# Four output units added onto their residual rows by DMA, and more turns for the recurrent units

## The chip, the cores and the metric

The kernel runs on one core of a Trainium2 chip. The metric is the device time of one execution in microseconds. Three timed executions of the kernel before gave 1637.43, 1637.99 and 1639.67.

## The reference

A two-layer encoder over 512 tokens of width 2048, all in float32:

```
for layer in (0, 1):
    hn = rmsnorm(x, norm_gain[layer])
    out = even_layer(hn) if layer == 0 else odd_layer(hn)
    x = x + out
return rmsnorm(x, final_gain)

even_layer: proj = hn @ w_in -> q, k, v, g_attn, x_lru, g_lru
    attn = softmax attention, 8 heads in 2 groups, rotary positions
    xc   = convolution of width 4 over x_lru, + bias
    y    = rg_lru(xc, forward) + rg_lru(xc, backward)   # gates r, i; h = a*h + u along the tokens
    out  = concat(attn * silu(g_attn), y * silu(g_lru)) @ w_out
odd_layer:  proj = hn @ w_in -> q, k, v, o, z, gates
    h    = mlstm(forward) + mlstm(backward)             # 8 heads, chunks of 128 tokens
    out  = (rmsnorm(sigmoid(o) * h, norm_gain) * silu(z)) @ w_out
```

## The kernel before

Features lie on the 128 partitions and tokens along a row, so x is 16 feature tiles of 128 x 512, handled in eight chunks of two. Every float32 operand is split into a rounded high part and a rest (`split`, L152: ScalarE casts the high part, VectorE subtracts for the low part), and a product is three matmuls (`mm3`).

*Steps and loads.* The whole program is one list of groups (`run_steps`), each of eight chunks of the contraction. `ahead` loads weight chunks (`raw`, three buffers, all on the SP queue) and splits them (`wh`, `wl`, four buffers) a few chunks before TensorE uses them. A group's `pre` runs with the splits, its `evac` empties the PSUM banks behind the last chunk, and its `after` adds new side work.

*Lanes.* Side work (attention, recurrent units, mLSTM heads) is written as generators in two lanes; `pump(lane)` runs the next step of a lane. In a plain group lane 0 gets a turn behind bank 1 of each chunk (or behind the banks in `turns`), and lane 1 gets `pace` turns at a chunk's end. Lane 1 of layer 1 holds the four recurrent units (`lru_gen`), each of 13 steps: two convolutions, four gate products, four steps of elementwise work, and the scans (L919 to L923). The groups of layer 1 run in the order keys and values, Q[0], L[0], L[1], Q[1], GL[0], GL[1], GA[0], GA[1], where Q are the queries, L the recurrent inputs, GL the gates of the recurrent units and GA those of attention; then four output groups. `mix_split` needs the gated values in the order 0, 1, 4, 5, 6, 7, 2, 3, where 4 to 7 are the recurrent units; where one is not there, `drain_until` runs the lane's rest at once. A value that is ready before its gate is parked in memory (`mixd`) and loaded again.

*Layer 2's output projection.* Output rows come as eight units of 256 features. Group 0 makes units 0 and 1 plainly (`out2_evac`). Units 2 to 6 are seven-product groups (`run_w7`, lay `W7`): POOL forms sums of weight blocks (`w7s`, L361), both parts are split, and per chunk 21 matmuls of 256 columns go to four banks; `w7_plain` (L483 to L493) combines these in VectorE while the next unit runs, one piece a chunk, from the deque `later`. For each of these units the residual rows are loaded from `x2d` (`res_pre`, L951), added (L1365), squared (L1393), summed over the features into one accumulator `acc` (L1395, on POOL for tiles 4 to 13), scaled with the final gain (L1375) and parked in memory (`x3_store`, L1380), since the operands of the projection fill 32 of 37 large buffers. Unit 6 is kept.

*The last group* (`run_last`) loads the parked units back (L1407) and makes unit 7 in two forms: as rows for tokens 0 to 255 and as columns for tokens 256 to 511, in two halves u = 0 and 1. Behind the rows, `rows_norm` forms the factor of tokens 0 to 255 from `acc` and the last squares, spreads it over the partitions by a matmul (`rB`) and scales and stores all units; `columns_norm` does the same for each half of the other tokens, with the squares of unit 7 taken along the row and those of the other features by `others`.

Instructions are put in order for each engine by the framework's scheduler, in program order with a simulated clock; `high_priority` moves some ahead.

Of the kernel before, what the change touches and what calls it, by code (L numbers as in the profile page):

```python
# [19 lines left out]
P = 128  # L20
# [7 lines left out]
NEG = -1e30  # L28
SLOT = 1032
O7, V7 = (0, 1, 2, 3), (0,)  # L30
PACE = 2
TURNS = (0, 1, 2)
STD = 'V1 V2 V3'
NSLOT = 37

PB_BA, PB_BX, PB_LAM, PB_CW, PB_CB = 0, 16, 32, 48, 80
# [5 lines left out]
class Builder:  # L42
# [255 lines left out]
    def run_steps(self, groups):  # L298
        self.steps = [(g, c) for g in groups for c in range(NCH)]
        self.raw, self.wsp = {}, {}  # L300
        self.nload = self.nsplit = 0
        self.ahead(0, 2, 1)
        i = 0
        for g in groups:
            if g["lay"] == "W7":
                self.run_w7(g, i)
                i += NCH
                continue
            if g["lay"] == "W7c":
                self.run_w7c(g, i)  # L310
                i += NCH
                continue
            g["ps"] = [None] * 4
            while self.later:
                self.evac_later()
            if g["lay"] == "last":
                self.run_last(g, i)
                i += NCH
                continue
            for c in range(NCH):  # L320
                self.ahead(i, 3, 2)
                g["c"] = c
                ws = self.wsp.pop(i)
                for b in range(g.get("nb", 4)):
                    if c == 0:
                        g["ps"][b] = self.bank.tile([P, 512], F32, tag="bulk", name=self.name("bk"))
                    self.bulk_mm(g, g["ps"][b], g["x"](c), ws, b, c)
                    if (c < NCH - 1 or b < 1 and "turns" in g) and b in g.get("turns", (1,)):
                        self.pump(0)
                    if c == NCH - 1 and b == 0 and g.get("mid"):  # L330
                        g["mid"]()
                if c == NCH - 1:
                    with self.tc.high_priority(offset=100):
                        for b in range(g.get("nb", 4)):
                            g["evac"](b, g["ps"][b])
                    if g.get("after"):
                        g["after"]()
                    self.pump(0)
                self.pump(1, g.get("pace", 1))
                i += 1  # L340


# [51 lines left out]
    def run_w7(self, g, i):  # L394
        beside = g["f"] % 2 == 0
        pool, tag = (self.bank, "bulk") if beside else (self.aux, "aux")
        if not beside:
            self.drain_until(0, lambda: not self.held)
        ps = [None] * 4

        def product(n, c):
            a, kind, q, b, hf = self.W7[n]
            wh, wl = self.wsp[i + c]
            xh, xl = g["x"](c)[kind]
            out = self.cols7(ps[b], b, hf)
            xh, xl = (t[:, q, :].rearrange("p (q s) -> p q s", q=2) for t in (xh, xl))
            last = c == NCH - 1 and (b == 3 or hf == 1)
            self.mm3(out, wh[:, a, :], wl[:, a, :], xh, xl, c == 0 and hf == 0, last)

        for c in range(NCH):  # L410
            self.ahead(i + c, 4, 3)
            if c == 0:
                ps = [pool.tile([P, 512], F32, tag=tag, name=self.name("s7")) for _ in range(4)]
            if g.get("apart") and c >= NCH - 2:
                if c == NCH - 1:
                    for b in (0, 1, 3, 2):
                        for k in (c - 1, c):
                            for n in range(7):
                                if self.W7[n][3] == b:
                                    product(n, k)  # L420
                        self.w7_plain(g, b, ps[b])
                    self.wsp.pop(i + c - 1)
                    self.wsp.pop(i + c)
                continue
            for n in range(7):
                product(n, c)
            if c == NCH - 1:
                self.later.extend(partial(self.w7_plain, g, b, ps[b]) for b in (0, 1, 3, 2))
            self.wsp.pop(i + c)
            if c < NCH - 1:  # L430
                self.evac_later()
            if beside and c % 3 == 1:
                self.pump(0)
        if g.get("after"):
            g["after"]()

# [549 lines left out]
class Layer2(Layer1):  # L986
# [368 lines left out]
    def out2_evac(self, b, ps):  # L1355
# [3 lines left out]
        if b % 2:  # L1359
            self.x3_store(b // 2)  # L1360

    def out2_7(self, i):
        def part(t, j):
            x3 = self.xres[i][:, j, :]
            self.nc.vector.tensor_add(x3, x3, t[:, j, :])  # L1365
            self.out2_scale(2 * i + j)
            if j and i < 6:
                self.x3_store(i)

        return lambda t: self.later.extend(partial(part, t, j) for j in range(2))  # L1370

    def out2_scale(self, k):
        x3 = self.xres[k // 2][:, k % 2, :]
# [25 lines left out]
    def run_last(self, g, i0):  # L1399
# [2 lines left out]
        nc, v = self.nc, self.nc.vector  # L1402
        for c in range(NCH):
            self.ahead(i0 + c, 1, 0)
        for n in sorted(self.x3d):
            self.xres[n] = self.slot2("xres")
            nc.sync.dma_start(out=self.xres[n], in_=self.x3d[n])  # L1407
        gf = self.slot("gfrow")[:, 0:256]
        nc.sync.dma_start(out=gf, in_=self.a["gf_row"].partition_broadcast(P))

# [37 lines left out]
                out=self.a["out"][2 * i * P:(2 * i + 2) * P, cs].rearrange("(j p) s -> p j s", p=P),  # L1448
                in_=self.xres[i][:, :, cs])

        def scale(n, i, cs, rb):
            x3 = self.xres[i][:, :, cs]
            eng, r = (nc.gpsimd, rb[1]) if i in (1, 4) else (v, rb[0])
            eng.tensor_tensor(out=x3, in0=x3, in1=r.unsqueeze(1).to_broadcast([P, 2, cs.stop - cs.start]),
                              op=ALU.mult)
            store(n, i, cs)

        def columns(u, between):
            ps = self.bank.tile([P, 512], F32, tag="bulk", name=self.name("bk"))[:, 0:256]
            ts = slice(u * P, (u + 1) * P)  # L1460
            for k in range(KT):
                if k in (1, 5):
                    next(between)
                wh, wl = self.wsp[i0 + k // 4 * 2]
                xh, xl = self.h_op(k // 2, k % 2, 1)
                self.mm3(ps, xh[:, ts], xl[:, ts], wh[:, k % 4, :], wl[:, k % 4, :], k == 0, k == KT - 1)
                if k == 0:
                    for j in range(2):
                        self.mm(ps[:, j * P:(j + 1) * P], self.xres[7][:, j, 256 + u * P:256 + (u + 1) * P],
                                self.ident, start=False, stop=False)  # L1470
            return ps

        def others(u):

# [6 lines left out]
        def columns_norm(u, ps, s):  # L1481
            t = self.slot("x3c")[:, 0:256]
            nc.scalar.activation(t, ps, AF.Square, accum_out=s[:, 1:2])
            v.scalar_tensor_tensor(out=s[:, 0:1], in0=s[:, 1:2], scalar=1.0 / D, in1=s[:, 0:1],
                                   op0=ALU.mult, op1=ALU.add)
            r = self.small(1, "r3c", 2)
            self.rsqrt_short(r, s[:, 0:1], 1)
            yield
            rb = spread(r, 1)
            cs = slice(256 + u * P, 256 + (u + 1) * P)  # L1490
            for i in range(7):
                scale(i, i, cs, rb)
                if i == 2:
                    v.scalar_tensor_tensor(out=t, in0=ps, scalar=r, in1=gf, op0=ALU.mult, op1=ALU.mult)
                    nc.sync.dma_start(out=self.a["outc"][u * P:(u + 1) * P, :], in_=t)
            yield

        step = rows_norm(rows())
        s = others(0)
        step = columns_norm(0, columns(0, step), s)  # L1500
        s = others(1)
        for _ in columns_norm(1, columns(1, step), s):
            pass


    def build(self):
# [49 lines left out]
        def after_lru(g):  # L1556
# [2 lines left out]
                add(1, self.lru_gen(2 * g + 1))  # L1559
            return f  # L1560

        L = [grp(w1, 2560 + 512 * g, "T", x1, self.xlru_evac(g), after=after_lru(g)) for g in range(2)]
        Q = [grp(w1, 512 * g, "tok", x1, self.q_evac(g), after=after_q(g)) for g in range(2)]
        GA = [grp(w1, 1536 + 512 * g, "T", x1, self.gate_evac(2 * g)) for g in range(2)]
        GL = [grp(w1, 3584 + 512 * g, "T", x1, self.gate_evac(4 + 2 * g)) for g in range(2)]
        groups += [Q[0], L[0], L[1], Q[1], GL[0], GL[1], GA[0], GA[1]]

        order = [0, 1, 4, 5, 6, 7, 2, 3]
# [29 lines left out]
        SQ = [s7(1024 * w + 256 * p, 2 * (p - 1) + w, lambda t, p=p, w=w: self.qk_store(p, w, t))  # L1598
              for p in range(1, 4) for w in range(2)]
        SZ = [s7(6144 + 256 * f, 6 + f, self.z7_evac(f)) for f in range(6)]  # L1600
        Z3 = grp(w2, 6144 + 1536, "T", x2, self.z_evac, turns=TURNS, pace=PACE)
        V = [grp(w2, 2048 + 512 * p, "tok", x2, self.v_evac(p), after=after_v(p)) for p in range(4)]
        O = [grp(w2, 4096 + 512 * p, "tok", x2, self.o_evac(p), after=lambda p=p: add(1, self.hT_gen(p)))
             for p in range(4)]
# [27 lines left out]
        def late2(c):  # L1632
            if c < NCH - 1:
                h_next()

        groups[-1]["pre"] = early2
        groups.append(grp(wo2, 0, "T", hx, self.out2_evac, turns=TURNS, pace=PACE,
                          pre=self.res_pre((0, 1), self.x2d, late2)))
        groups += [dict(w=wo2[:, 256 * i:256 * i + 256], lay="W7", f=i + 1, order=range(NCH), x=self.hs.__getitem__,
                        evac=self.out2_7(i), pre=self.res_pre((i,), self.x2d)) for i in range(2, 7)]  # L1640
        groups.append(dict(w=wo2[:, 1792:2048], lay="last", order=range(NCH), pre=self.res_pre((7,), self.x2d)))
        self.run_steps(groups)

# [95 lines left out]
```

## Time and profile before

| | |
|---|---|
| median of three executions | 1637.99 us |
| the profiled execution, its own time | 1640.25 us |
| span of its profile | 1638.2 us |
| TensorE busy | 1611.1 us, 98% |
| VectorE, ScalarE, POOL busy | 1137.2, 846.6, 751.7 us |
| mean granted clock of TensorE | 0.996 |

In the rows, PE is TensorE, PEld its weight loads, DVE VectorE, ACT ScalarE, POOL GpSimd and SP the SyncE queue; a q behind the name is the engine's queue, where DMAs are issued. A row of the waits gives the waiting instruction, what ended the wait, the total in us, how often, and the longest. A row of grouped instructions gives the count, the busy time, the mean in ns, and the idle time before them. A row of the timeline gives start, duration and what was done. Matmuls overlap in the pipeline, so their pace is read from start to start and not from the duration.

### The profile page before, as it was taken

What the parts mean: (1) busy time and instruction counts of PE and PEld (TensorE: products, weight loads), DVE (VectorE), ACT (ScalarE), POOL (GpSimd) and SP (SyncE); (2) the same over time, 40 slices, a digit from 0 to 9 for tenths busy, and PEclk for the clock granted to TensorE, in tenths of its full rate; (3) what the DMA queues carried; (4) which work ended last, traced back from release to release, by engine and by line L of the source; (5) the groups of instructions that cost most, each with busy time, mean ns of one, the idle gap of its engine ahead of it and who ended that gap; (6) DMA issues with size and microseconds to landing.
All of it is one profiled execution on the core that took longest, in us unless ns stands there. A gap on an engine that the chain in (4) does not pass through costs nothing.

```text
span 1638.2 us, 25397 instructions
## 1 busy us (share of the span) xinstructions
PE 1611.1 (98%) x9698; PEld 1423.2 (87%) x9698; DVE 1137.2 (69%) x1714; ACT 846.6 (52%) x1392; POOL 751.7 (46%) x728
## 2 busy tenths in 40 slices
PE   9999999999998999999999999999999999999997
PEld 7888888888887888889999999999988888878997
DVE  8755476856755333548998896666776676688995
ACT  6334665667663333434444444444566566565542
POOL 5220122302031111576688778888521312468881
PEclk9999999999999999999999999999999999999999
DMA  7433133322324446634444444444654344443346
GB/s 231 133 93 98 52 103 103 92 89 65 116 78 151 170 168 201 193 111 118 129 120 140 129 130 117 136 135 129 193 180 130 105 154 154 158 151 116 130 157 219
DMA packets 138842, 220.22 MB, mean 134 GB/s; under 512 B 9936, under 2 KB 62544, under 8 KB 138720
## 3 DMA queue, kind: packets, MB, share of 16 engines
q1 hardware_dynamic: 137488, 217.99, 42.4%
q8 instruction: 76, 1.25, 0.3%
q10 hardware_dynamic: 1232, 0.60, 0.1%
q14 instruction: 46, 0.38, 0.1%
HBM read 184.46 MB, written 34.11 MB: 133 GB/s over the span
## 4 chain that ended last, share of the span: by engine, by line
PE 83%; DVE 7%; POOL 3%; issue 2%; ACT 2%; DMA 2%; SPq 0%; DVEq 0%; POOLq 0%; ACTq 0%
PE bk L157 47%; PE s L157 26%; DVE wl L154 3%; PE PV L157 1%; PE lg L157 1%; PE nb L157 1%; PE nf L157 1%; PE S L157 1%; PE tr L160 1%; POOL w7s L361 1%; PE ST L157 1%; PE gt L157 0%; DMA raw<-in_odd_w_out_dram 0%; POOL hfb L1323 0%; DVE ltau L919 0%
## 5 line engine op out<-in xcount | busy, mean ns | idle before, releaser
L154 DVE TENSOR_TENSOR wl<-raw,wh 128x1024 fp32r<-128x1024 f32 (+3 forms) x333 | 367.3, 1105 | 254.9 <-ACT wh L153 252.8
L153 ACT CAST wh<-raw 128x1024 fp32r<-128x1024 f32 (+3 forms) x333 | 265.7, 799 | 397.7 <-PE bk L157 189.9
L361 POOL TENSOR_TENSOR w7s<-raw 128x256 f32<-128x256 f32 x216 | 222.3, 1048 | 101.7 <-DMA raw<-in_odd_w_in_dram 55.3
L154 DVE TENSOR_TENSOR wl<-w7s,wh 128x512 fp32r<-128x512 f32 (+1 forms) x176 | 206.7, 1174 | 7.5 <-ACT wh L153 7.5
L157 PE MATMUL s<-th,wl 128*128 128x256 f32 x544 | 154.0, 283 | 4.4 <-DVE wl L154 4.4
L157 PE MATMUL s<-tl,wh 128*128 128x256 f32 x544 | 152.7, 281 | 0.0
L157 PE MATMUL s<-th,wh 128*128 128x256 f32 x544 | 152.5, 280 | 0.0
L157 PE MATMUL bk<-xh,wh 128*128 128x512 f32 x384 | 151.7, 395 | 0.0
L157 PE MATMUL bk<-xl,wh 128*128 128x512 f32 x384 | 151.3, 394 | 0.0
L157 PE MATMUL bk<-xh,wl 128*128 128x512 f32 x384 | 151.1, 393 | 0.0
L153 ACT CAST wh<-w7s 128x512 fp32r<-128x512 f32 (+1 forms) x176 | 125.7, 714 | 45.5 <-POOL w7s L361 45.4
L899 POOL TENSOR_TENSOR li<-li,xc 128x512 f32<-128x512 f32 x16 | 21.6, 1371 | 213.3 <-ACT li L891 213.3
L361 POOL TENSOR_TENSOR w7s<-w7s,raw 128x256 f32<-128x256 f32 x108 | 117.8, 1091 | 0.0
L157 PE MATMUL s<-bh,wl 128*128 128x256 f32 x408 | 115.1, 282 | 2.0 <-DVE wl L154 2.0
L157 PE MATMUL s<-bh,wh 128*128 128x256 f32 x408 | 115.2, 282 | 0.0
L157 PE MATMUL s<-bl,wh 128*128 128x256 f32 x408 | 114.6, 281 | 0.0
L361 POOL TENSOR_TENSOR w7s<-raw,w7s 128x256 f32<-128x256 f32 x108 | 105.0, 972 | 7.8
L157 PEld LDWEIGHTS s<-th,wl 128*128 128x128 f32 x544 | 102.4, 188 | 6.8 <-DVE wl L154 6.8
L157 PE MATMUL bk<-oh,wh 128*128 128x512 f32 x256 | 101.8, 398 | 5.0 <-DVE gate L805 5.0
L157 PEld LDWEIGHTS s<-tl,wh 128*128 128x128 f32 x544 | 102.5, 189 | 0.0
L157 PEld LDWEIGHTS s<-th,wh 128*128 128x128 f32 x544 | 102.5, 188 | 0.0
L157 PE MATMUL bk<-oh,wl 128*128 128x512 f32 x256 | 101.5, 396 | 0.0
(342 smaller groups left out, 4537.7 us busy)
## 6 DMA issues: line engine op xcount, KB each, us to landing
raw<-in_odd_w_in_dram SPq DMA_DIRECT2D x120, 512.0 KB, 3.9
raw<-in_even_w_in_dram SPq DMA_DIRECT2D x71, 512.0 KB, 3.7
raw<-in_even_w_out_dram SPq DMA_DIRECT2D x32, 512.0 KB, 3.6
raw<-in_odd_w_out_dram SPq DMA_DIRECT2D x32, 512.0 KB, 3.7
xres<-in_xT_dram SPq DMA_DIRECT2D x8, 512.0 KB, 6.7
x2d<-xres SPq DMA_DIRECT2D x8, 512.0 KB, 4.9
xgd<-xg SPq DMA_DIRECT2D x8, 512.0 KB, 4.5
xr<-xgd SPq DMA_DIRECT2D x8, 512.0 KB, 6.6
```

What stands on the lines that cost most here:

```text
L153: self.nc.scalar.copy(h, x)
L154: (eng or self.nc.vector).tensor_tensor(out=l, in0=x, in1=h.bitcast(F32), op=ALU.subtract)
L157: self.nc.tensor.matmul(out, a, b, start=start, stop=stop)
L160: self.nc.tensor.transpose(out, x, ident)
L361: po.tensor_tensor(out=s[:, :, q, :], in0=x, in1=y, op=op)
L899: nc.gpsimd.tensor_tensor(out=ii[j][:, d, :], in0=ii[j][:, d, :], in1=xc[:, j, :], op=ALU.mult)
```

## The change

1. *Turns.* A new key `more` gives lane 1 a turn behind bank 1 of the first `more` chunks of a group, besides the one at each chunk's end. Q[1], GL[0] and GL[1] get five; the last gate group of layer 2 (Z3) and group 0 of the output projection get eight, in place of `pace=2`.
2. *Accumulating DMA.* Units 2 to 5 no longer load their residual rows. Their combined tile is added onto the rows of `x2d` in memory by a DMA that POOL issues (`out2_onto`). From chunk 3 of unit 6 on, units 0 to 4 are loaded back, one a chunk (`x3_load`); unit 5 is loaded in the last group.
3. *Squares and scales.* The rows of units 2 to 5 are squared and scaled in the last group (`late_square`, `late_scale`), in two halves of 256 tokens; VectorE adds the squares of the first half to `acc`, POOL those of the second.
4. *The end.* `others` moves into the column products, at step 10 of 16. The factor of a column half is formed at high priority. In the second half the seven scaled tiles go into two packed buffers, and two stores take the place of seven.

```diff
-PACE = 2
+LATE = (2, 3, 4, 5)
...
+                    if b == 1 and c % 8 < g.get("more", 0):
+                        self.pump(1)
...
-                self.pump(1, g.get("pace", 1))
+                self.pump(1)
...
+            if g.get("each"):
+                g["each"](c)
...
+    def out2_onto(self, i):
+        return lambda t: self.nc.gpsimd.dma_start(out=self.rows2(self.x2d, i), in_=t, accum_op=ALU.add)
+
     def out2_7(self, i):
...
-            if j and i < 6:
-                self.x3_store(i)
...
+    def x3_load(self, i):
+        self.xres[i] = self.slot2("xres")
+        self.nc.sync.dma_start(out=self.xres[i], in_=self.x3d[i] if i in self.x3d else self.rows2(self.x2d, i))
+
+    def late_square(self, i, cs):
+        sq = self.half("sq3").rearrange("p (j s) -> p j s", j=2)
+        self.nc.scalar.activation(sq, self.xres[i][:, :, cs], AF.Square)
+        eng = self.nc.gpsimd if cs.start else self.nc.vector
+        for j in range(2):
+            eng.tensor_tensor(out=self.acc[:, cs], in0=self.acc[:, cs], in1=sq[:, j, :], op=ALU.add)
+
+    def late_scale(self, i, cs):
+        for k in (2 * i, 2 * i + 1):
+            x3 = self.xres[i][:, k % 2, cs]
+            self.nc.scalar.activation(x3, x3, AF.Copy, scale=self.pb[:, PB_GF + k:PB_GF + k + 1])
...
+        for n in range(7):
+            if n not in self.xres:
+                self.x3_load(n)
...
+                if k == 10:
+                    s = others(u)
...
+            with self.tc.high_priority(offset=100):
+                v.scalar_tensor_tensor(out=s[:, 0:1], in0=s[:, 1:2], scalar=1.0 / D, in1=s[:, 0:1],
+                                       op0=ALU.mult, op1=ALU.add)
+                self.rsqrt_short(r, s[:, 0:1], 1)
...
+            packed = [self.slot("x3p")[:, 0:1024].rearrange("p (i j s) -> p i j s", i=4, j=2) for _ in range(2 * u)]
             for i in range(7):
-                scale(i, i, cs, rb)
+                scale(i, i, cs, rb, packed[i // 4][:, i % 4] if u else None)
+                if u and i in (3, 6):
+                    (nc.scalar if i == 3 else nc.sync).dma_start(
+                        out=self.a["out"][i // 4 * 1024:(i + 1) * 256, cs].rearrange("(k p) s -> p k s", p=P),
+                        in_=packed[i // 4][:, 0:i % 4 + 1].rearrange("p i j s -> p (i j) s"))
...
+        h0, h1 = slice(0, 256), slice(256, 512)
+        for cs in (h0, h1):
+            for n in LATE:
+                self.late_square(n, cs)
+        for n in LATE:
+            self.late_scale(n, h0)
         step = rows_norm(rows())
...
+        for n in LATE:
+            self.late_scale(n, h1)
+        step = columns_norm(0, *columns(0, step))
+        for _ in columns_norm(1, *columns(1, step)):
...
-        Q = [grp(w1, 512 * g, "tok", x1, self.q_evac(g), after=after_q(g)) for g in range(2)]
+        Q = [grp(w1, 512 * g, "tok", x1, self.q_evac(g), after=after_q(g), more=5 * g) for g in range(2)]
-        GL = [grp(w1, 3584 + 512 * g, "T", x1, self.gate_evac(4 + 2 * g)) for g in range(2)]
+        GL = [grp(w1, 3584 + 512 * g, "T", x1, self.gate_evac(4 + 2 * g), more=5) for g in range(2)]
...
-        Z3 = grp(w2, 6144 + 1536, "T", x2, self.z_evac, turns=TURNS, pace=PACE)
+        Z3 = grp(w2, 6144 + 1536, "T", x2, self.z_evac, turns=TURNS, more=NCH)
...
+        groups += [u7(i, self.out2_onto(i)) for i in LATE]
+        groups.append(u7(6, self.out2_7(6), pre=self.res_pre((6,), self.x2d),
+                         each=lambda c: self.x3_load(c - 3) if c > 2 else None))
```

More of the change, by code (lines that the diff above doesn't have):

```diff
@@ L1366, in part, with rows2 @@
             self.out2_scale(2 * i + j)
-            if j and i < 6:
-                self.x3_store(i)
         return lambda t: self.later.extend(partial(part, t, j) for j in range(2))
+    def rows2(self, d, i):
+        return d[2 * i * P:(2 * i + 2) * P, :].rearrange("(j p) s -> p j s", p=P)
+    def x3_load(self, i):
[11 more added lines that the diff above has]
+            self.nc.scalar.activation(x3, x3, AF.Copy, scale=self.pb[:, PB_GF + k:PB_GF + k + 1])
     def out2_scale(self, k):
@@ L1404, in run_last @@
             self.ahead(i0 + c, 1, 0)
-        for n in sorted(self.x3d):
-            self.xres[n] = self.slot2("xres")
-            nc.sync.dma_start(out=self.xres[n], in_=self.x3d[n])
+        for n in range(7):
+            if n not in self.xres:
+                self.x3_load(n)
         gf = self.slot("gfrow")[:, 0:256]
@@ L1449, in store, with scale @@
                 in_=self.xres[i][:, :, cs])
-        def scale(n, i, cs, rb):
+        def scale(n, i, cs, rb, to=None):
             x3 = self.xres[i][:, :, cs]
             eng, r = (nc.gpsimd, rb[1]) if i in (1, 4) else (v, rb[0])
-            eng.tensor_tensor(out=x3, in0=x3, in1=r.unsqueeze(1).to_broadcast([P, 2, cs.stop - cs.start]),
-                              op=ALU.mult)
-            store(n, i, cs)
+            eng.tensor_tensor(out=x3 if to is None else to, in0=x3, op=ALU.mult,
+                              in1=r.unsqueeze(1).to_broadcast([P, 2, cs.stop - cs.start]))
+            if to is None:
+                store(n, i, cs)
         def columns(u, between):
@@ L1470, in columns @@
                                 self.ident, start=False, stop=False)
-            return ps
+            return ps, s
         def others(u):
@@ L1483, in columns_norm @@
             nc.scalar.activation(t, ps, AF.Square, accum_out=s[:, 1:2])
-            v.scalar_tensor_tensor(out=s[:, 0:1], in0=s[:, 1:2], scalar=1.0 / D, in1=s[:, 0:1],
-                                   op0=ALU.mult, op1=ALU.add)
             r = self.small(1, "r3c", 2)
-            self.rsqrt_short(r, s[:, 0:1], 1)
+            with self.tc.high_priority(offset=100):
+                v.scalar_tensor_tensor(out=s[:, 0:1], in0=s[:, 1:2], scalar=1.0 / D, in1=s[:, 0:1],
+                                       op0=ALU.mult, op1=ALU.add)
+                self.rsqrt_short(r, s[:, 0:1], 1)
             yield
@@ L1496, in columns_norm @@
             yield
+        h0, h1 = slice(0, 256), slice(256, 512)
[4 more added lines that the diff above has]
+            self.late_scale(n, h0)
         step = rows_norm(rows())
[L1499 to L1502, printed above, removed]
+        for n in LATE:
+            self.late_scale(n, h1)
+        step = columns_norm(0, *columns(0, step))
+        for _ in columns_norm(1, *columns(1, step)):
             pass
@@ L1636, in build, with u7 @@
         groups[-1]["pre"] = early2
-        groups.append(grp(wo2, 0, "T", hx, self.out2_evac, turns=TURNS, pace=PACE,
+        groups.append(grp(wo2, 0, "T", hx, self.out2_evac, turns=TURNS, more=NCH,
                           pre=self.res_pre((0, 1), self.x2d, late2)))
-        groups += [dict(w=wo2[:, 256 * i:256 * i + 256], lay="W7", f=i + 1, order=range(NCH), x=self.hs.__getitem__,
-                        evac=self.out2_7(i), pre=self.res_pre((i,), self.x2d)) for i in range(2, 7)]
+        def u7(i, evac, **kw):
+            return dict(w=wo2[:, 256 * i:256 * i + 256], lay="W7", f=i + 1, order=range(NCH), x=self.hs.__getitem__,
+                        evac=evac, **kw)
+        groups += [u7(i, self.out2_onto(i)) for i in LATE]
+        groups.append(u7(6, self.out2_7(6), pre=self.res_pre((6,), self.x2d),
+                         each=lambda c: self.x3_load(c - 3) if c > 2 else None))
         groups.append(dict(w=wo2[:, 1792:2048], lay="last", order=range(NCH), pre=self.res_pre((7,), self.x2d)))
```

## The prediction

> **What bounds the kernel now.** I read the page first, then TensorE's waits, then the chain of waits and the timelines around the two places that it shows, and last the windows by stage.
>
> ```profile
> span 1638.2 us, 25397 instructions
> PE   1611.1 (98%) x9698; PEld 1423.2 (87%) x9698; DVE 1137.2 (69%) x1714; ACT 846.6 (52%) x1392; POOL 751.7 (46%) x728
> PE s L157 <- DVE wl L154: 6.5, 11, 1.1
> PE bk L157 <- DVE gate L805: 5.0, 1, 5.0
> PE rB L157 <- DVE diag L596: 3.1, 2, 2.9
> PE nf L157 <- ACT hfb L1320: 1.4, 1, 1.4
> PE hT L160 <- ACT hfb L1190: 1.1, 3, 0.5
> ```
>
> TensorE is the bound: 1611.1 of 1638.2 us. A change can win only idle TensorE time, stretches of lower clock, and the tail behind the last matmul. One wait of 5.0 us stands alone, where the last gate group of layer 1 hands over to its output projection:
>
> ```profile
> 498.01 0.40 PE L157 MATMUL bk<-xh,wl 128*128 128x512 f32 x1
> 503.39 0.77 PE L157 MATMUL bk<-oh,wh 128*128 128x512 f32 x1 [4.99 <-DVE gate L805]
> 487.91 3.40 DVE L919 TENSOR_TENSOR_SCAN ltau<-lr,li 128x512 f32<-128x512 f32 x1 [2.31 <-POOL li L914]
> 498.01 1.23 DVE L828 TENSOR_TENSOR y<-y,gate 128x1024 f32<-128x1024 f32 x1 [1.19 <-POOL y L923]
> 502.56 2.48 DVE L805 TENSOR_TENSOR gate<-bk,rB 128x512 f32<-128x512 f32 x4
> 498.00:503.40 5.40, 0.41 (x3) 0.04 (x1) 5.38 (x6) 2.45 (x3) 0.00 (x0) 0.74 0.55 170
> 503.40:507.40 4.00, 4.00 (x10) 3.14 (x11) 2.78 (x4) 3.24 (x5) 0.00 (x0) 0.50 0.99 377
> ```
>
> The first two rows are the gap: start to start 5.38 us. VectorE spends the time before it on the last recurrent unit's scans (L919 and the line after it), its gating (L828), splits, and only then empties the PSUM banks (L805). In the windows (length, then PE, PEld, DVE, ACT, POOL, the granted clock, DMA) the clock falls to 0.50 right behind the gap, for 4.0 us of matmuls. The stall costs 5.38 - 0.23 (a normal step; 24 take 5.55 us in the chain row below) = 5.15, plus 4.0 x (1 - 0.50) = 2.0: **7.1 us**.
>
> The Trainium skill (TensorE: Matmul & The Clock Gate, Part 1) says that an idle window of about 3.4 us drops TensorE to half clock; the trace agrees, with 0.50 behind a 5.38 us gap.
>
> The second place is layer 2's output projection, units 2 to 6:
>
> ```profile
> 1495.01 0.28 PE L157 MATMUL s<-bl,wh 128*128 128x256 f32 x1
> 1497.03 0.28 PE L157 MATMUL s<-th,wh 128*128 128x256 f32 x1
> 1495.20:1601.70 106.50, 102.47 (x839) 100.11 (x839) 100.48 (x121) 56.23 (x105) 83.18 (x78) 1.00 0.48 159
> L154 DVE TENSOR_TENSOR wl<-w7s,wh 128x512 fp32r<-128x512 f32 x38 | 43.3, 1140 | 1.8 <-ACT wh L153 1.8
> L154 DVE TENSOR_TENSOR wl<-raw,wh 128x384 fp32r<-128x384 f32 x38 | 35.1, 924 | 1.5 <-ACT wh L153 1.5
> L361 POOL TENSOR_TENSOR w7s<-raw 128x256 f32<-128x256 f32 x35 | 35.3, 1030 | 14.7 <-DMA x3d<-xres 5.5 <-DMA raw<-in_odd_w_out_dram 4.3 <-DVE wl L154 3.7
> L361 POOL TENSOR_TENSOR w7s<-w7s,raw 128x256 f32<-128x256 f32 x18 | 20.0, 1112 | 0.0
> L361 POOL TENSOR_TENSOR w7s<-raw,w7s 128x256 f32<-128x256 f32 x18 | 17.3, 962 | 1.4
> L1365 DVE TENSOR_TENSOR xres<-xres,x 128x512 f32<-128x512 f32 x10 | 11.8, 1185 | 0.0
> L1395 POOL TENSOR_TENSOR acc<-acc,sq 128x512 f32<-128x512 f32 x10 | 15.8, 1575 | 14.2 <-ACT sq L1393 14.1
> L493 DVE TENSOR_TENSOR x<-x,s 128x256 f32<-128x256 f32 x5 | 2.1, 413 | 0.0
> L1393 ACT ACTIVATE sq<-xres 128x512 f32<-128x512 f32 x13 | 8.1, 628 | 15.0 <-DVE xres L1365 15.0
> ```
>
> Seventeen steps between the first two rows take 2.02 us, 0.119 each, so 839 matmuls need 99.8 us of the 106.5: **6.7 us lost**, while VectorE is 94% busy. Per unit TensorE needs 168 x 0.119 = 20.0 us. VectorE has 16 weight splits at a mean (43.3 + 35.1)/76 = 1.03, 16.5 us, seven combining steps at about 0.41, 2.9, and two residual adds, 2.4: 21.8, over TensorE's pace. POOL has 16 weight sums at (35.3 + 20.0 + 17.3)/71 = 1.02, 16.4, and two square sums, 3.2: 19.6, right at the pace.
>
> **The change, part by part.** *Turns.* A recurrent unit has 13 steps, four units 52. Before, lane 1 gets one turn a chunk: 1 at the end of the first recurrent group, then 8 a group; by chunk 5 of the last gate group 46 are spent, and the remaining six are poured out at once. The change adds 5 each in the second query group and the two recurrent gate groups: 1 + 8 + 13 + 13 + 13 = 48, and the 52nd comes in chunk 3 of the first attention gate group, twelve chunks ahead of the handover:
>
> ```profile
> 469.35 5.55 PE bk L157 x24
> 300.00:350.00 50.00, 50.00 (x236) 41.02 (x236) 40.93 (x65) 27.86 (x42) 7.18 (x5) 1.00 0.39 116
> 60.00:498.00 438.00, 437.23 (x2067) 359.58 (x2066) 279.64 (x417) 255.31 (x357) 94.49 (x80) 1.00 0.29 88
> ```
>
> A chunk of 24 matmuls takes at least 5.55 us, so the scans end some 67 us early and the stall goes whole: -7.1. What is packed tighter is VectorE: 279.64 of 438 us is 64%, and the busiest stretch now, 40.93 of 50, hides wholly under TensorE. Two steps in a chunk can delay a split or an attention transpose; between 60 and 498 us TensorE idles 0.8 us now. I take +1.0 for that (bounds 0 and 3, a few scans of the 3.40 row). Two more recurrent outputs finish before their gate and go out to memory and back, 512 KB each way, off every chain: 0 (if a reload came late at the gate: one landing, 4.3 us by the x3d row below). Term: **-6.1**.
>
> *Four units by accumulating DMA.* Units 2 to 5 lose residual load, two adds, two squares, two square sums, two scales and store. VectorE falls to 19.4 a unit, under 20.0. SP loses eight transfers that stood between weight loads: SPq waited for the x3d stores, and POOL for the weights behind them.
>
> ```profile
> SPq L951 <- DMA x3d<-xres: 12.6, 3, 4.7
> 1562.32 2.30 POOL L361 TENSOR_TENSOR w7s<-raw 128x256 f32<-128x256 f32 x2 [2.87 <-DMA raw<-in_odd_w_out_dram]
> x3d<-xres SPq DMA_DIRECT2D x6, 512.0 KB, 4.3
> 1550.59 0.34 SPq L1380 DMA_DIRECT2D x3d<-xres  x1
> ```
>
> What POOL pays to issue one such DMA no row shows: none is issued from POOL here. It has 20.0 - 16.4 = 3.6 us a unit before its sums set the pace; bounds: 0.34 us (SPq's issue row) and 4.3 (if it held POOL until landing, x3d row). The issue waits for the unit's last combining step (L493), and the next chunks' weight sums stand behind it, as they stood behind the square sums. I take 2 us, nearer the issue row, since a queue does not wait for landing. Then the 6.7 us goes but for 0.8 at the entry (group 0's evacuation, unchanged) and 1.2 of leftovers: **-4.7** (bounds -6.7 and +2: at 4.3 us POOL is 0.7 over in three units).
>
> In the Trainium skill, DMA: Bandwidth & Descriptors (Anatomy of one DMA) fits 2.0 us plus bytes/436e3 to a transfer from this queue: by estimate 3.2 us for 512 KB; held for that long POOL still fits its 3.6, and the sum stays.
>
> *Turns in the last gate group and output group 0.* The same two turns a chunk, apart instead of together. The hT and nf waits above (2.5 us) may shrink: **-0.5** (bounds -2.5 and +1).
>
> *The tail.* Loads of the parked units move under unit 6 (the stage's DMA share is 0.48 above); unit 5's comes last.
>
> ```profile
> 1608.59 2.66 POOL L1395 TENSOR_TENSOR acc<-acc,sq 128x512 f32<-128x512 f32 x2 [12.76 <-ACT sq L1393]
> 1613.90 0.43 DVE L1395 TENSOR_TENSOR acc<-acc,sq 128x256 f32<-128x256 f32 x1
> 1618.57 0.70 PE L157 MATMUL rB<-diag,ones 128*128 128x256 f32 x2 [0.21 <-DVE diag L596]
> 1601.70:1613.20 11.50, 11.50 (x100) 11.50 (x99) 6.26 (x12) 4.47 (x7) 2.58 (x2) 1.00 0.80 314
> 1628.31 0.19 ACT L1483 ACTIVATION_READ_ACCUMULATOR x3c<-bk 128x1 f32 x1
> 1629.21 0.15 DVE L1484 SCALAR_TENSOR_TENSOR rowss<-rowss 128x1 f32<-128x1 f32 x1
> 1632.45:1636.50 4.05, 0.00 (x0) 0.00 (x0) 1.29 (x4) 0.00 (x0) 1.01 (x2) 0.50 0.98 290
> ```
>
> The square sums of units 2 to 5 now come behind unit 6's on POOL, which end at 1611.25. Eight half adds on VectorE at 0.43 are 3.4: 1614.7 instead of 1613.9, and with the wait at the row factor nearly closed (0.21) TensorE feels it: +0.8 (bounds 0, and 4 if unit 5's load lands late, by one 4.3 us landing). Eight more on POOL, at its 1.02 a sum, end at 1619.4; the matmul that reads them now stands at step 10 of the first column product, behind the row factor's 1618.57: within the same bound. ScalarE squares and scales the same elements as before, later (8 squares at 0.63, 5.0 us, and as much scaling): its free 7.0 us in the window above and what it has under unit 6 hide that, 0, or it is part of the 4. The high priority takes 1629.21 - 1628.5 = 0.7 off the last factor: -0.6. Packing 7 stores into 2: DMA already runs at share 0.98 to the end, and the first packed store must wait for four scales: +0.2 (bounds -1 and +1). Term: **+0.4**.
>
> Sum: -6.1 - 4.7 - 0.5 + 0.4 = **-10.9**. The profiled execution took 1640.25 with a span of 1638.2 and becomes 1629.4; it stood 2.26 above the median of 1637.99, so I say **1627**.
>
> **Rivals.** *(a) POOL takes the bound:* issuing costs over 3.6 us or wakes late, the units run at the old 106.5: 1637.99 - 6.1 - 0.5 + 0.4 = **1631.8**. For: POOL at 19.6 of 20.0 now; against: it loses 3.2 of that.
> *(b) The recurrent stall moves:* new waits of several us among the gate groups, with the lower clock behind one: -10.9 + 6.1 = **1633.2**. For: the 3.40 us scan; against: 64% load.
> *(c) Late squares hold the tail:* +4 instead of +0.8: **1630.3**. For: a single accumulator in program order; against: units 2 to 4 load early.
> *(d) Slower:* the accumulating issue holds POOL for x us. It costs 3 (x - 3.6) over TensorE's pace in the three units whose successors need sums; the stage gets 99.8 + 0.8 + that. At x = 9 it is 116.8, +10.3: 1637.99 - 6.1 - 0.5 + 0.4 + 10.3 = **1642.1**. It decides above x = 7.6, where the sum is nil. For: no row prices it; against: POOL's dearest instruction in the stage is 1.6 us.
> The Trainium skill (SBUF, The "DVE blocks DMA" trap) lets VectorE's two-port operations starve such descriptor writing, which is this mechanism; its section Who interferes with whom exempts TENSOR_TENSOR, the form of every VectorE row quoted in the stage, so it does not raise the chance.
>
> **How the numbers follow.** Forecast 0.5, (a) 0.18, (b) 0.1, (c) 0.14, (d) 0.04, no effect anywhere 0.04. A measurement tells about 0.2%, 3.3 us, from no change: faster 0.88 (all but the last two and 0.04 of (b), which lies close to it), same 0.08, slower 0.04. The forecast's own range is 1624 to 1630; with (a), (b) and (c) 1623 to 1634.
>
> **What would show it.** Right: no gap and clock 1.00 around the handover; no scan after the first attention gate group; units 2 to 6 in 101 to 102 us; POOL's DMA rows under 3 us; stc at the row factor within 1 us of its old distance from unit 6's end. Wrong: weight sums waiting on POOL's own queue, a gap over 3 us among the gate groups, or squares of unit 5 waiting for their load.

## The result, and the profile after

The changed kernel is slower: 1651.63 us, median of six executions (1648.95 to 1653.67), against 1638.86 us (1637.43 to 1639.88) for six executions of the kernel before. The ratio is 1.0077, with a 95% interval from 1.0064 to 1.0090. The prediction said 1627 us and faster, so it was wrong in sign. The profiled execution, 1648.95 us, is the fastest of the six; it is read against the 1640.25 us of before.

TensorE's busy time has hardly moved. These are lines of the page of the changed kernel:

```profile
span 1647.2 us, 25420 instructions
PE 1612.9 (98%) x9698; PEld 1425.4 (87%) x9698; DVE 1125.2 (68%) x1714; ACT 847.3 (51%) x1400; POOL 754.4 (46%) x732
```

The span is 9.0 us longer. TensorE's waits in the changed kernel (the waiting instruction, what ended the wait, then us in total, times, longest) show new ones in place of the old:

```profile
PE lg L157 <- DVE qT L154: 6.1, 1, 6.1
PE stc L157 <- DVE acc L1421: 5.5, 1, 5.5
PE tr L160 <- ACT pm L793: 5.2, 2, 5.1
PE S L157 <- ACT attn L774: 1.8, 1, 1.8
```

The handover wait (5.0, "bk <- DVE gate") is gone, and most of the losses of units 2 to 6 ("s <- DVE wl", 6.5) too. Three waits of layer 1 are new (`lg`, `tr`, `S`), and one at the end (`stc`). Their places in TensorE's timeline of the changed kernel, with the first product of layer 1's output projection in the last row:

```profile
309.18 1.65 PE L157 MATMUL lg<-xchl,lws 128*128 128x512 f32 x3 [6.14 <-DVE qT L154]
353.15 1.11 PE L160 MATMUL tr<-ident,pm 128*128 128x128 f32 x4 [5.06 <-ACT pm L793]
414.70 0.50 PE L157 MATMUL S<-kTh,qT 128*128 128x512 f32 x1 [1.79 <-ACT attn L774]
515.31 0.39 PE L157 MATMUL bk<-oh,wh 128*128 128x512 f32 x1
```

That product began at 503.39 before, followed by half clock that cost another 2.0 us; now it begins at 515.31 at full clock. Layer 1 has thus lost 11.9 - 2.0 = 9.9 us, although the handover's 7.1 us are gone: 17.0 us are new. The windows of the changed kernel (length, then PE, PEld, DVE, ACT, POOL, the granted clock, DMA) say why:

```profile
284.00:309.00 25.00, 18.60 (x80) 14.28 (x78) 23.90 (x40) 8.98 (x12) 12.92 (x9) 0.93 0.35 107
309.20:312.20 3.00, 3.00 (x7) 2.40 (x8) 3.00 (x5) 1.07 (x2) 0.00 (x0) 0.52 0.44 158
341.00:353.00 12.00, 7.09 (x31) 5.42 (x29) 11.40 (x13) 8.54 (x12) 5.26 (x3) 1.00 0.17 49
353.20:356.60 3.40, 3.40 (x11) 2.88 (x12) 1.93 (x3) 3.40 (x5) 0.43 (x1) 0.52 0.00 0
1502.10:1601.60 99.50, 99.50 (x842) 99.50 (x841) 81.37 (x113) 46.94 (x88) 71.58 (x74) 1.00 0.58 167
```

The same first stretch in the kernel before:

```profile
284.00:309.00 25.00, 25.00 (x116) 20.40 (x115) 18.94 (x20) 18.03 (x20) 16.89 (x11) 1.00 0.22 64
```

VectorE is busy 23.90 of 25 us ahead of the first stall and 11.40 of 12 ahead of the second, and behind each TensorE runs at clock 0.52 for about 3 us. Two rows of VectorE's timeline of the changed kernel show what meets there, a recurrent unit's convolution (L862) and the query rotation (L666):

```profile
293.24 2.73 DVE L862 SCALAR_TENSOR_TENSOR xc<-xpad,pb,xc 128x512 f32<-128x512 f32 x4
...
302.43 0.69 DVE L666 TENSOR_TENSOR qf<-qf,ropet 128x512 f32<-128x512 f32 x1
```

The three waits (6.1, 5.1, 1.8) and the half clock behind the first two, 3.0 and 3.4 us at 0.52, make 16.1 of the 17.0 us.

The last row of the windows of the changed kernel is cut at the first and last matmul of units 2 to 6: 99.50 us instead of 106.7, all of it busy, so 7.2 us are won there. The stage begins 7.2 us late (1502.10 against 1494.9) and ends where it ended before (1601.6 against 1601.7). Everything that the span lost net lies behind it. The chain of waits of the changed kernel over the end, in order of time:

```profile
1587.19 10.54 DMA x2d<-x
1597.75 0.36 SPq L1383
...
1598.21 6.42 DMA raw<-in_odd_w_out_dram
...
1613.60 1.89 ACT sq L1388 x4
...
1617.76 3.19 ACT xres L1396 x8
1620.95 0.31 ACT sq L1419
...
1621.29 0.43 DVE acc L1421
...
1623.70 5.33 PE bk L157 x24
```

Unit 5's accumulating DMA takes 10.54 us. SyncE's queue holds a reload that waits for it, and the last two weight loads stand behind that reload. It is the reload of unit 4, whose own DMA had been issued at 1566.91 and had landed 5.9 us later. So it does not wait for its rows; most likely it waits for the large buffer that unit 5's tile gives up when it lands, but this was not tried. Beside this landing the reloads moved under unit 6 fill the DMA engines, with a share of 0.98 (last but one number):

```profile
1587.20:1597.70 10.50, 10.50 (x91) 10.50 (x91) 5.61 (x9) 3.70 (x7) 1.22 (x1) 1.00 0.98 255
```

Then come the late squares (L1388) and scales (L1396), in ScalarE's order ahead of the last rows' squares (L1419). The two timelines show the copy that begins unit 6's evacuation, the late sums and the product of the row factor. First the changed kernel, then the kernel before:

```profile
1605.68 0.58 ACT L487 COPY w7u<-s 128x512 f32<-128x512 f32 x1
1614.55 5.40 DVE L1391 TENSOR_TENSOR acc<-acc,sq 128x256 f32<-128x256 f32 x8 [2.85 <-POOL acc L1421]
1628.82 0.99 PE L157 MATMUL rB<-diag,ones 128*128 128x256 f32 x2
```

```profile
1602.07 0.58 ACT L483 COPY w7u<-s 128x512 f32<-128x512 f32 x1
```

Before, the last sum ahead of the row factor began at 1613.90 and the factor's product `rB` at 1618.57; the span ended at 1638.2. From unit 6's end on, the stretches were 0.4 (to the copy), 11.8 (to the last sum), 4.7 (to `rB`) and 19.6 us (to the end), 36.5 in all. They are now 4.1, 15.6, 7.5 and 18.4, in all 45.6. So the tail is 9.1 us longer: +3.7 for weights behind a reload, +3.8 for late squares, sums and scales, +2.8 for the half clock behind the 5.5 us wait, -1.2 at the end. In the trace, +7.2 to unit 2, -7.2 in the units and +9.1 in the tail make the 9.0 of the span, but for rounding.

### The profile page after: what moved, and what is told of

It is laid out like the page before. It is cut to its first block, busy times and chain, and to the rows that moved or that the text cites. A ratio compares the mean times of both kernels' runs of the same rounds, so it can differ in the third digit from the quotient of the medians.

```text
span 1647.2 us, 25420 instructions
## 1 busy us (share of the span) xinstructions
PE 1612.9 (98%) x9698; PEld 1425.4 (87%) x9698; DVE 1125.2 (68%) x1714; ACT 847.3 (51%) x1400; POOL 754.4 (46%) x732
## 4 chain that ended last, share of the span: by engine, by line
PE 81%; DVE 9%; ACT 4%; DMA 3%; issue 2%; POOL 2%; SPq 0%; DVEq 0%; ACTq 0%; POOLq 0%
PE bk L157 44%; PE s L157 28%; DVE wl L154 2%; PE nb L157 1%; PE nf L157 1%; PE lg L157 1%; PE ST L157 1%; POOL w7s L363 1%; PE PV L157 1%; PE S L157 1%; DMA x2d<-x 1%; PE tr L160 1%; DVE ltau L912 1%; DMA raw<-in_odd_w_out_dram 1%; DMA hTr<-hTd 1%
## 5 line engine op out<-in xcount | busy, mean ns | idle before, releaser
L154 DVE TENSOR_TENSOR wl<-raw,wh 128x1024 fp32r<-128x1024 f32 (+3 forms) x333 | 361.7, 1088 | 294.4 <-ACT wh L153 293.2
L363 POOL TENSOR_TENSOR w7s<-raw 128x256 f32<-128x256 f32 x216 | 226.7, 1069 | 91.8 <-DMA raw<-in_odd_w_in_dram 53.6
L157 PE MATMUL bk<-ol,wh 128*128 128x512 f32 x256 | 100.8, 394 | 0.0
```

What stands on the lines that cost most here:

```text
L154: (eng or self.nc.vector).tensor_tensor(out=l, in0=x, in1=h.bitcast(F32), op=ALU.subtract)
L157: self.nc.tensor.matmul(out, a, b, start=start, stop=stop)
L363: po.tensor_tensor(out=s[:, :, q, :], in0=x, in1=y, op=op)
```

## The experiments

Each was executed 4 to 11 times; the time of before is the median on the same chip (1638.5 to 1639.1 us). The stages below are cut at the first product of unit 2, at the first one behind unit 6, and at the end of the span.

**The extra turns of layer 1 alone.** The kernel before with

```diff
+                    if b == 1 and c % 8 < g.get("more", 0):
+                        self.pump(1)
-... self.q_evac(g), after=after_q(g))
+... self.q_evac(g), after=after_q(g), more=5 * g)
-... self.gate_evac(4 + 2 * g))
+... self.gate_evac(4 + 2 * g), more=5)
```

> The kernel before with one part of the change alone: five more turns of the recurrent lane in the second query group and in each recurrent gate group of layer 1. Theory (these turns cost more than they give: they put the recurrent units' convolutions, products and scans on VectorE beside the query rotation and the gate evacuations): the first matmul of layer 2's output units comes 7.2 us later than before, as in the changed kernel, so the time is about 1638.9 + 7 = 1646 us, with gaps of 5 to 7 us among the gate groups. Rival (the lateness at that place comes from the turns of the last gate group and output group 0 in layer 2, or from the profile's own clock): within 3 us of 1639.

Measured: 1651.73 us (1649.68 to 1654.4), 13.2 us slower, ratio 1.0084 (1.0070 to 1.0097). The theory holds in kind; its 7 us were too mild. TensorE's waits in this kernel:

```profile
PE lg L157 <- DVE qT L154: 6.1, 1, 6.1
PE s L157 <- DVE wl L154: 5.3, 10, 0.8
PE tr L160 <- ACT pm L791: 5.1, 1, 5.1
```

They are the changed kernel's stalls beside the old loss of the output units. The first product of the output projection comes at 516.0 us and the output units begin at 1505.9, 11.0 us later than before. The profiled execution of the changed kernel, the fastest of its six, stands at the mild end of what these turns cost.

**The changed kernel without them.** `more` is taken out of the groups of layer 1.

> The changed kernel without the fifteen extra turns of layer 1; all else as changed. Theory: the handover stall of 5.4 us is back, the new gaps among the gate groups are gone; units 2 to 6 stay at 99.5 us (-7.2 against before) and the tail at 45.7 us (+9.2), so about 1639 - 7.2 + 9.2 = 1641 us, some 8 to 10 us under the changed kernel. Rival (the tail's lateness follows from the turns): tail back at 37 us, 1632 us.

Measured: 1639.95 us (1638.65 to 1640.56), ratio 1.0010 (1.0001 to 1.0019). The theory said 1641 and holds; the rival is out. The units take 99.3 us, the tail 44.8, and the waits name both ends:

```profile
PE bk L157 <- DVE gate L809: 5.0, 1, 5.0
PE stc L157 <- DVE acc L1421: 4.5, 1, 4.5
```

Turns +13.2 and all the rest +1.4 add to 14.6 us; the whole change measured 12.8. The loss belongs to the turns of layer 1, and the rest of the change gives its gain back in the tail.

**Extra turns in another place.** Without those, but eight in the first attention gate group: `GA ... more=8 * (1 - g)`.

> The changed kernel with the extra turns in another place: none in the query and recurrent gate groups, eight in the first attention gate group, where no query rotation and no split of it is left. The recurrent units still end before the last gate group's evacuation. Theory (the place of the turns, not their number, makes the stalls): handover stall gone, no new gap over 3 us, start of the output units 7 us earlier than before, about 1651.6 - 14 = 1637 us. Rival (any packing of the recurrent units moves the stall): gaps of 5 us appear in the attention gate groups, 1643 us or more.

Measured: 1644.77 us, a miss by 8 us: better than the changed kernel by 7 but with a new stall. The timeline of this kernel shows its mechanism in VectorE's, ScalarE's and POOL's rows, then TensorE's wait:

```profile
465.61 3.41 DVE L923 TENSOR_TENSOR_SCAN ltau<-lr,li 128x512 f32<-128x512 f32 x1 [3.59 <-POOL li L918]
468.95 1.19 DVE L925 TENSOR_TENSOR_SCAN ltau<-lr,li 128x512 f32<-128x512 f32 x1
471.18 2.28 DVE L154 TENSOR_TENSOR wl<-raw,wh 128x1024 fp32r<-128x1024 f32 x1
460.73 1.28 ACT L917 ACT_TABLE_LOAD   x1
463.16 4.78 POOL L918 TENSOR_TENSOR li<-li,ltau 128x1024 f32<-128x1024 f32 x2 [4.96 <-ACT ltau L917]
```

```profile
PE bk L157 <- DVE wl L154: 5.9, 2, 5.2
```

VectorE idles 3.59 us with a scan at the head of its queue: the scan waits for POOL's product, which waits for ScalarE's roots behind a table load. The weight split that TensorE needs stands behind the scan. Here VectorE is not full; the step came too soon behind the step that feeds it.

**One step a chunk, none of them empty.** Of the 13 steps of a recurrent unit two are empty, a bare `yield` each. In the kernel before, they are left out (52 steps become 44).

```diff
                                op0=ALU.add, op1=ALU.mult)
         yield
-        yield
...
             nc.gpsimd.tensor_tensor(out=ii[j], in0=ii[j], in1=tau[j], op=ALU.mult)
         yield
-        yield
```

> The kernel before with one edit: the two empty steps of each recurrent unit (a bare yield after the exponentials and after the square roots) are left out, 44 steps instead of 52, still one step a chunk; no extra turn anywhere. The last scans come some 40 us earlier than before. Theory (two working steps in one chunk overfill VectorE; one a chunk does not): the handover gap of 5.4 us goes, no new gap over 2 us, about 1638.5 - 7 = 1631.5 us. Rival (whatever ends the recurrent units earlier moves the stall to another place): new gaps of 5 us among the gate groups, 1640 us or more.

Measured: 1638.97 us, no change (0.9991 to 1.0008), a miss by 7.5 us; the rival's new stalls came, but smaller (waits of 2.3, 1.9 and 0.9 us). The handover stall is gone from its place, but the gain is lost between 220 and 400 us, so "two working steps in a chunk" was not the whole cause. A wait, two rows of VectorE's timeline and a window of this kernel:

```profile
PE bk L157 <- DVE gate L805: 2.3, 1, 2.3
```

```profile
318.90 4.05 DVE L858 SCALAR_TENSOR_TENSOR xc<-xpad,pb,xc 128x512 f32<-128x512 f32 x6
...
328.15 1.88 DVE L805 TENSOR_TENSOR gate<-bk,rB 128x512 f32<-128x512 f32 x3
```

```profile
329.50:332.90 3.40, 3.40 (x10) 2.66 (x9) 3.30 (x5) 3.02 (x5) 0.00 (x0) 0.52 0.62 197
```

The steps now meet other chunk ends: the first gate group's evacuation (L805) stands behind six convolution instructions and their splits, and 2.3 us of idle are followed by 3.4 us of half clock.

**The tail: a reload behind the weights.** The changed kernel with unit 4's reload behind the last two weight loads on SyncE's queue.

```diff
-                         each=lambda c: self.x3_load(c - 3) if c > 2 else None))
+                         each=lambda c: self.x3_load(c - 3) if 2 < c < 7 else None))
```

> The changed kernel with the reload of unit 4 moved on SyncE's queue from ahead of the last two weight loads to behind them; the turns as changed. Theory (those weight loads stood behind the landing of unit 5's accumulating DMA): they are issued some 5 us earlier, the copy of unit 6's evacuation follows unit 6 directly (0.4 us after it instead of 4), and the tail shrinks by 4 to 6 us: 1646 us. Rival (the tail is set by the late squares and sums whenever the weights come): within 2 us of 1651.6.

Measured: 1649.63 us (1647.12 to 1649.91), 2.0 us under the changed kernel: where the rival's range ends. The intervals of the two ratios overlap (1.0054 to 1.0079 against 1.0064 to 1.0090), so the size is uncertain. Against unit 6's end the weight loads are issued 5.3 us earlier (8.7 us ahead of it instead of 3.4), as the theory said, but take longer to land, 9.83 us instead of 6.42; chain of waits:

```profile
1596.16 9.83 DMA raw<-in_odd_w_out_dram
```

Five loads of rows were issued in the 8 us ahead of them. The copy follows unit 6 after 2.2 us instead of 4.1, and the tail is 42.7 us instead of 45.6.

**The tail: order only.** On the kernel without the extra turns: units 5, 0 and 1 are reloaded behind the weights, and `late_scale` stands behind the last rows.

> The changed kernel without the fifteen extra turns, and with two orders of the tail changed: the reloads of unit 5 and of units 0 and 1 stand behind the last weight loads (units 2 to 4 stay ahead of them), and ScalarE scales the late units behind the last unit's rows. The late squares and sums stay where they were. Theory (order on two queues, not the work, made the tail long): the copy of unit 6's evacuation comes within 1 us of unit 6's end, the gap ahead of the row sums falls from 4.8 us to 2 us or less, tail 45 to about 40 us, 1635 us. Rival (the eight late half sums on VectorE and the landing of unit 5 set it): within 2 us of the 1640 us of the run without extra turns.

Measured: 1637.87 us (1634.62 to 1640.04), 2.1 us under the kernel without turns, tail 43.1 us. The theory missed by 3 us; the rival is nearer. The copy follows unit 6 after 0.1 us (3.1 in the kernel without turns), as the theory said; 1.3 of these 3.0 us are lost again behind it. The chain of waits still runs through the late sums, and the half clock follows:

```profile
1602.14 0.43 DVE acc L1391
...
1605.95 0.78 DVE acc L1391
...
1611.12 5.33 PE bk L157 x24
```

**The tail: the late work taken off it.** On the kernel without the extra turns: three units by DMA, squared, summed and scaled under unit 6, and unit 5 as before, but kept in its buffer. `late_square` now handles whole rows, with all sums on POOL, and its calls and those of `late_scale` in the last group are gone (not shown).

```diff
-LATE = (2, 3, 4, 5)
+LATE = (2, 3, 4)
...
+        groups.append(u7(5, self.out2_7(5), pre=self.res_pre((5,), self.x2d)))
+        def early_late(c):
+            if c < 3:
+                self.x3_load(LATE[c])
+            elif c < 6:
+                self.late_square(LATE[c - 3], slice(0, S))
+            if c > 3:
+                for n in LATE[(c - 4):(c - 3)]:
+                    self.late_scale(n, slice(0, S))
```

> The changed kernel without the fifteen extra turns, with three units (2, 3 and 4) added onto their rows by DMA and unit 5 as in the kernel before, but kept in its buffer. Units 2 to 4 are loaded in the first three chunks of unit 6 and squared, summed (all on POOL) and scaled in the chunks behind; only units 0 and 1 are loaded behind the last weights. Theory (the tail grew by unit 5's landing and by late sums on the chain): tail back at 35 to 37 us, units 2 to 6 at 100 to 102 us since unit 6 has its two adds again, about 1632 us. Rival (loads early in unit 6 hold the weight loads behind them): unit 6 loses 3 us or more, 1636 us or more.

Measured: 1632.73 us (1631.25 to 1635.41), ratio 0.9965 (0.9951 to 0.9978): faster than before by 6 us and than the kernel without turns by 7.2. Its windows, cut at the output units and the tail, and POOL's last late sums:

```profile
1490.91:1592.56 101.65, 100.08 (x842) 99.49 (x840) 93.12 (x114) 55.93 (x105) 81.14 (x81) 1.00 0.53 158
1592.56:1629.48 36.92, 26.70 (x220) 25.88 (x218) 20.45 (x63) 9.26 (x19) 7.98 (x8) 0.91 0.50 161
```

```profile
1586.77 3.19 POOL L1390 TENSOR_TENSOR acc<-acc,sq 128x512 f32<-128x512 f32 x2
```

The tail is 36.9 us (36.5 before), the late sums end at 1589.96, ahead of the last unit, and the units take 2.3 us more than without turns, with unit 5's adds back in VectorE's queue. The theory holds. The edit changes several things at once (one DMA unit less, reloads earlier, squares under unit 6), and which of them won how much was not tried. Of the 8.7 us between the two profiles, 3.2 stand ahead of unit 2, where the edit changes nothing; the tail gives 7.9 and the units take 2.3.

**This tail with the recurrent units without empty steps.** The two edits above together.

> The kernel of three units by DMA with the early squares, together with the recurrent units without empty steps. If the two gains are independent they add: about 1632 - 7 = 1625 us. If the earlier scans meet something else in layer 1, 1632 us.

Measured: 1632.89 us (1632.67 to 1635.69), nothing beyond the tail's gain; the earlier scans lose in layer 1 what they win, as alone.

**Two turns, in the last gate group only.** The kernel of three units by DMA, without the fifteen turns; `more` is now a set of chunks.

```diff
-                    if b == 1 and c % 8 < g.get("more", 0):
+                    if b == 1 and c in g.get("more", ()):
...
+        GA = [grp(..., self.gate_evac(2 * g), more=(0, 1) if g else ()) for g in range(2)]
```

> The kernel of three units by DMA with the early squares, with two extra turns only: one each in the first two chunks of the last attention gate group, where the last recurrent unit is at its four gate products, which ask VectorE for two short additions each. Nothing moves before 445 us, so every other step of the recurrent units meets the same neighbours as in the kernel before, and the last unit's products end two chunks (11 us) earlier. Theory (a stall comes where a scan stands in VectorE's queue waiting for POOL and ScalarE, with a weight split or a transpose's eviction behind it; the handover needs its last unit only 5 us earlier): handover gap under 1 us, no new gap over 2 us, about 1632.7 - 7 = 1626 us. Rival (earlier always stalls elsewhere): 1632 us or more.

Measured: 1627.16 us (1626.98 to 1628.07), ratio to before 0.9929 (0.9916 to 0.9943). The theory holds; the rival is out. The output projection of layer 1 now begins with no stall (timeline), and the windows keep the gains:

```profile
498.55 0.47 PE L157 MATMUL bk<-oh,wh 128*128 128x512 f32 x1 [0.17 <-DVE gate L809]
```

```profile
1487.38:1588.57 101.19, 99.61 (x841) 99.20 (x840) 92.80 (x114) 55.82 (x105) 82.12 (x81) 1.00 0.53 159
1588.57:1625.32 36.75, 26.70 (x220) 25.86 (x218) 20.43 (x63) 9.36 (x19) 7.96 (x8) 0.92 0.51 162
```

**A third turn, in chunk 3 (`more=(0, 1, 3)`).**

> As the run with two extra turns, with a third in the fourth chunk of that group, so that only the scans are left to be poured out in the sixth. Theory: the same as with two, 1626 us, or up to 3 us more, since the roots then follow closer behind the exponentials and VectorE waits for POOL with weight splits behind it. Rival: as before.

Measured: 1626.97 us (1626.58 to 1628.12), the same as with two.

**The two turns in the kernel before, alone.**

> The kernel before with nothing but the two extra turns in the first two chunks of the last attention gate group. If the handover stall is worth what the run with three units by DMA lost by them (1632.7 to 1627.2, 5.6 us) to 7.1 us, 1638.9 minus that: 1632 to 1633.5 us; what lies between this run and the one with both (some 5 us) is then the accumulating DMAs, the early squares and the turns of layer 2. Rival (the handover hides part of the DMA units' loss, or the reverse): outside 1631 to 1635 us.

Measured: 1632.11 us (1631.25 to 1633.27), ratio 0.9962 (0.9950 to 0.9975): the handover stall is worth 6.5 us. All else in the kernel with two turns (the DMA units with early squares above all, the turns of layer 2 and the end) gives another 5.0.

**The old end in the fastest kernel.** Ordinary priority for the last factor, seven single stores.

> The kernel with three units by DMA and two extra turns, with the end as in the kernel before: the last column factor at ordinary priority and seven single stores for the last 128 rows instead of two packed ones. Theory (in the changed kernel the stretch from the row factor's product to the end was 1.4 us shorter, 18.2 against 19.6): 1 to 1.5 us slower than with the packed end, 1628.5 us. Rival (the store queue decides the end whichever way): within 0.5 us of 1627.2.

Measured: 1627.45 us (1626.62 to 1628.1) against 1627.16: no difference that can be measured. The rival holds. The 1.2 us by which the changed kernel's last stretch was shorter do not show in the time.

## Why the prediction was wrong

*Turns (-6.1; measured +13.2 alone).* The stall was read rightly: it is worth 6.5 us, and two turns take it away whole. The step that failed is "VectorE: 279.64 of 438 us is 64%, and the busiest stretch now, 40.93 of 50, hides wholly under TensorE", and the +1.0 with bounds 0 and 3 taken from it. A share over 438 us says nothing of the 25 us in which query rotation, convolutions, scans and splits met (23.90 busy). The bounds priced "a few scans", not what stands behind them in an in-order queue, nor the half clock that followed two of the three stalls; the prediction had itself priced 2.0 us for that at the handover. Moved steps were also taken at their old durations, and packing puts them beside POOL: ahead of the second stall one weight split of 128x1024 took 3.43 us, and the next 1.21.

Rival (b), "the recurrent stall moves", happened, at three times its price: (b) only took the gain of 6.1 us away, and the new waits of 6.1, 5.1 and 1.8 us with their half clock cost that and 13 us more. The argument against it, "64% load", was the same failed step. The signal named for it, a gap over 3 us among the gate groups, is what the trace shows.

*Accumulating DMA (-4.7; -7.2 in the trace).* Right, and better than said: the leftovers of 0.8 and 1.2 us did not appear. The five profiles with four such units show 99.3 to 99.6 us for this stage, the four with none 105.3 to 106.8; no run has the DMA units alone. The unknown price, POOL's issue, was 1.2 to 1.3 us (taken 2; bounds 0.34 and 4.3). Rivals (a) and (d) are out: the kernel became slower, as (d) had it, but not by (d)'s mechanism. POOL's rows of the changed kernel:

```profile
1528.51 1.34 POOL L1368 DMA_DIRECT2D x2d<-x  x1
1587.19 1.23 POOL L1368 DMA_DIRECT2D x2d<-x  x1
```

*Turns in layer 2 (-0.5).* Not settled: the 1.4 us `nf` wait of before is gone in the changed kernel, but with two turns in layer 1 the output units begin at 1487.1 us without these turns and at 1487.4 with them. From the first product of layer 1's output projection to unit 2, profiles of kernels without the handover stall show 988.5 to 989.9 us without these turns and 986.8 to 990.0 with them.

*The tail (+0.4; +9.1 in the trace).* The terms failed one by one. The landing was bounded by "one 4.3 us landing" of a plain store; the accumulating one took 10.54, beside the reloads that the change itself put there. The loads "under unit 6" were counted as hidden at a DMA share of 0.48; they raised it to 0.98, and the weight loads behind them on SyncE's queue came late. Eight half sums "at 0.43 are 3.4" measured 5.40: the first four took 0.42 to 0.43 each, the last four 0.76 to 0.83, with POOL's own sums beside them. The ScalarE work was taken to hide in free time, without its order: eight scales, 3.29 us in all, stand ahead of the last rows' squares. And with the wait at the sums at 5.5 us, the half clock came on top. Rival (c), the late squares, happened too: 3.8 us of the tail's 9.1, near its +4, and the 2.8 of half clock behind them; the 3.7 for the weights lie outside it. The priority (-0.6) and the packing (+0.2) are nothing measurable. The order of queues explains about 2 us of the tail's loss by experiment; taking the late work off the tail gave 7.2.

In sum, 1627 us was within reach of the parts: with the late work under unit 6 and two well-placed turns they give 1627.2. That is another kernel, and that it meets the forecast to 0.2 us is luck. What the forecast did not price is what the change as it stands puts behind each moved step.

## What to carry to other kernels

Where steps are moved onto an engine with in-order issue, look at the share of that engine in the target stretch plus what is added, and write down what stands behind each moved step in its queue and what the step itself waits for. To clear a late producer, pull forward the cheap steps just ahead of it, and only so many as the stall needs; everything else keeps its neighbours. Work that is deferred to free a busy stage must end under that stage's last part and not behind it, and a reload that waits for another DMA does not belong ahead of loads that do not.

## What the runs showed of the hardware

The four accumulating DMAs of 512 KB landed after 5.9 to 10.5 us, median 6.2; the longest is the one beside the reloads. Plain stores of the same size to the same tensor, at other times, took 4.3. The first row is of the four DMAs, the second of the DMA issues (count, size, median us to landing), both of the changed kernel:

```profile
DMA to landing us min/median/max: 5.9/6.2/10.5
x2d<-xres SPq DMA_DIRECT2D x8, 512.0 KB, 4.3
```

The Trainium skill (DMA: Bandwidth & Descriptors, Anatomy of one DMA) fits about 3.2 us to this size on this path, by estimate; the trace does not agree.

A scan of 128x512 took 3.41 us beside POOL's product and 1.19 right behind it (rows above). The Trainium skill (SBUF — State Buffer, Who interferes with whom) lets a VectorE instruction with two inputs from SBUF contend with POOL's reads; the trace agrees, at a factor of 2.9.

Half clock (0.52) followed idle waits of 6.1, 5.1 and even 2.3 us; behind the wait of 1.79 us at 414.70 the matmuls keep their full pace. The Trainium skill (TensorE: Matmul & The Clock Gate, Part 1) speaks of an idle window of about 3.4 us; here a shorter one was enough.
